# A hybrid retention and S5 step on one core: row order of the first loop, the norm's broadcast, and where the Toeplitz area is cleared

## The chip, the cores and the metric

The kernel runs on one core of one Trainium2 chip. The metric is the device time of one execution in microseconds (us), the median of several runs; the span is the time from the first to the last instruction in one profiled execution. Engines are called PE (matrix products), DVE (VectorE), ACT (ScalarE), POOL (GpSimd) and SP (SyncE, which only issues transfers here). Transfers are issued on the queues of SP, ACT and POOL.

## What is computed

One inference step of one layer, in float32, for a prompt of 1024 tokens and 8 single sample tokens, together 1032 token columns:

```python
h = rmsnorm(x, g_pre)                       # over d_model = 2048
q, k, v, za, ub, zb, ga, gb = split(h @ w_in)
ya, s_ret_new = retention(q, k, v, pos, s_ret)          # 8 heads of 128, chunks of 128
ya = (ya * silu(za)) @ w_pa
yb, s_re, s_im = s5(ub, ...)                # 64 groups of 16 channels, 64 complex states each
yb = (yb * silu(zb)) @ w_pb
out = (sigmoid(ga) * ya + sigmoid(gb) * yb) @ w_out
y = x + rmsnorm(out, g_post)
```

The outputs are y for both groups of tokens and the new states of the retention and of the S5 branch.

## The kernel before

All activations lie transposed: 128 channels on the partitions, tokens along the free axis. `xT` is x in 16 row tiles of 128 x 1032 (`KD` = 16). Each float32 operand is split into a high part, a rounded copy made by ACT, and a low part, the difference made by DVE; a product is the sum of three products of such parts (function `three`, lines 227 to 229, and line 952 in the main loop).

**First loop** (from line 382). It takes the row tiles k = 0 to 15. For each, SP loads the row (three buffers `xr`), ACT casts it times `g_pre` and DVE makes the low part; ACT squares the row (three buffers `sq`) and DVE adds the squares to `ssq`. PE at once multiplies the row with two column tiles of `w_in` (`M_UB`, `M_UB + 1`), three thirds of the tokens each. The 1/rms factor `rstd` isn't known yet, so these two results are kept unscaled and scaled later (`scale_ub`).

**The norm** (`first_rms`, `rms_bcast`). PE sums `ssq` over the partitions into a 128 x 9 tile, DVE adds epsilon, POOL takes the power -1/2, DVE multiplies an identity by the result (tile `st`, line 306), and PE multiplies a constant matrix with it, which broadcasts `rstd` to all partitions; DVE copies it out (line 317). Four 128-token chunks are done at a time, in three rounds.

**The forms** (`build_forms`). The main loop multiplies 2 x 2 blocks with seven products instead of eight, and needs seven combinations ("forms") of the scaled rows for each half of K: `u1`, `v1`, `v2` are pieces of the scaled rows, `t1` to `t4` are sums and differences of them, made in four `fo` buffers. They are stored to memory (`fm_d`) and read again later. For `kh` = 0 this works on rows 0 to 7 in four pairs (j, j + 4): POOL loads the rows again (buffers `fx`), DVE scales them (line 428) and makes the `t` forms, ACT issues the seven stores (line 438). For `kh` = 1 it does so with rows 8 to 15 in steps 1 to 3 of the main loop.

**Order of work.** `slot()` runs the next piece, up to a `yield`, of the first generator in the list `bg`; the projections call it at fixed places. While `linear` computes the third and fourth column tiles, there are four slots for each quarter of K: one behind each third of the tokens, and one behind the quarter. The high and low weights (`whi`, `wlo`) rotate through three pairs of tiles, `a`, `b` and `c`; the weights of the next quarter are asked for at the start of a quarter (`fetch_w`). The order on each engine is fixed before the run by a list scheduler that goes by priority (program order), readiness and a model of costs, so an instruction that depends on little can stand earlier in its engine's queue than in the program. `issue_after` keeps the pieces of a slot behind the last weight cast, weight difference or matmul of that engine. Each engine works through its queue in order.

**Main loop.** Steps of seven products of 24 matmuls each; `at(g, f)` runs f behind product g. `fetch(s + 1)` asks on SP's queue for the weights of the next step, in product 1 of a step; there are seven buffers `wr`.

**S5.** From step `B0 + 3` = 9 the S5 parameters are computed (`s5_params`), from step `B0 + 6` = 12 the 16 batches of four groups (`s5_all`, with `s5_mats`, `s5_phase`, `s5_toep` and others). A batch builds Toeplitz matrices by writing kernel rows into `t_d` in memory at staggered offsets and reading them back as 128 x 128 blocks; the part that stays zero, 112 columns of each row, must be cleared first. `s5_mats` does this for each batch: POOL clears a tile `zz` (line 621) and stores it, broadcast, to the batch's rows (line 622). All batches use the same place for `zz`. `s5_mats` also loads the batch's coefficients `bc` on POOL's queue (line 618), which DVE uses first in line 626. DVE in addition evacuates PE's accumulators, into `u2`, `u3` and others.

Of the kernel before, what the change touches and what calls it, by code (L numbers as in the profile page):

```python
# [79 lines left out]
def emit(ctx, tc, I, O):  # L80
# [27 lines left out]
    def st_tile():  # L108
        return stage_of["pool"].tile([128, stage_of["w"]], F32, name="st")
# [114 lines left out]
    def three(ps, w, i, x, t0, t1, first, last):  # L224
        wh, wl = w
        xh, xl = x
        T.matmul(ps, wh[:, i, :], xh[:, t0:t1], start=first, stop=False)  # L227
        T.matmul(ps, wh[:, i, :], xl[:, t0:t1], start=False, stop=False)  # L228
        anchor["p"] = T.matmul(ps, wl[:, i, :], xh[:, t0:t1], start=False, stop=last).ins  # L229
# [6 lines left out]
    def misc():  # L236
        return banks_of["pms"].tile([128, 512], F32, name="misc")
# [87 lines left out]
    def x_of(k):  # L325
        return xs[k][:, 0, :], xs[k][:, 1, :]
# [48 lines left out]
    ubw = ubstack.enter_context(tc.tile_pool(name="ubw", bufs=3))  # L375
    rm = ubstack.enter_context(tc.tile_pool(name="rm", bufs=1))
    ssq = rm.tile([128, TOK], F32, name="ssq")

    with tc.tile_pool(name="start", bufs=3) as sp:
        banks = [[mmbank() for _ in range(3)], [mmbank(), mmbank(), misc()]]  # L380
        w = None
        sqs = deque()
        for k in range(KD):
            xr = sp.tile([128, TOK], F32, name="xr")
            xh, xl = x_of(k)
            parts = THIRDS[0:3] if k == 0 else [(0, TOK)]
            for n, (a, b) in enumerate(parts):
                nc.sync.dma_start(xr[:, a:b], I["xT"][k, :, a:b])
                if k % 4 == 0 and n == 0:
                    w = [wquarter(w_in, M_UB, k // 4)]  # L390
                if k % 4 == 0 and n == len(parts) - 1:
                    w.append(wquarter(w_in, M_UB + 1, k // 4))
                A.activation(xh[:, a:b], xr[:, a:b], AF.Copy, scale=gpre[:, k:k + 1])
                V.scalar_tensor_tensor(xl[:, a:b], xr[:, a:b], gpre[:, k:k + 1], xh[:, a:b].bitcast(F32), ALU.mult, ALU.subtract)
            if k == 0:
                A.activation(ssq, xr, AF.Square)
            else:
                sqs.append(sp.tile([128, TOK], F32, name="sq", bufs=3))
                A.activation(sqs[-1], xr, AF.Square)
            for j in range(2):  # L400
                for t, (t0, t1) in enumerate(THIRDS[0:3]):
                    three(banks[j][t][:, 0:t1 - t0], w[j], k % 4, x_of(k), t0, t1, k == 0, k == KD - 1)
            if k > 1:
# [8 lines left out]
    def build_forms(kh, pool, fxs, fos, pre, after=()):  # L412
        raw = {}

        def load(j):
            for n in range(2):
                k = 8 * kh + j + 4 * n
                raw[k] = pool.tile([128, TOK], F32, name="fx", bufs=fxs)
                P.dma_start(raw[k], I["xT"][k])

        for j in range(pre):
            load(j)
        yield
        for j in range(4):
            t = {}
            for n, k in (("u", 8 * kh + j), ("v", 8 * kh + 4 + j)):
                r = raw.pop(k)
                V.scalar_tensor_tensor(r, r, gpre[:, k:k + 1], rstd, ALU.mult, ALU.mult)
                t[n + "1"], t[n + "2"] = r[:, 0:HT], r[:, HT:TOK]
            yield  # L430
            for n, a, b, op in (("t1", "u1", "u2", ALU.subtract), ("t3", "u2", "v2", ALU.subtract),
                                ("t2", "v2", "t1", ALU.add), ("t4", "v1", "t2", ALU.subtract)):
                t[n] = pool.tile([128, HT], F32, name="fo", bufs=fos)
                tt(t[n], t[a], t[b], op)
                if n == "t3":
                    yield
            for p, n in enumerate(FORMS):
                A.dma_start(fm_d[kh, p, j], t[n])
            yield
            if j and j + pre - 1 < 4:  # L440
                load(j + pre - 1)
            if j < len(after):
                after[j]()
            yield

    def first_rms():
        yield
        yield from rms_bcast(ssq, rstd, rm, 1)

    fb = ubstack.enter_context(tc.tile_pool(name="fb", bufs=1))  # L450
    forms_a = build_forms(0, fb, 6, 4, 3, (lambda: scale_ub(0), lambda: scale_ub(1)))
    next(forms_a)
    bg.append(first_rms())
    bg.append(forms_a)
    todo.extend((w_in, m, kq) for m in (M_UB + 2, M_UB + 3) for kq in range(4))
    todo.append((w_in, 16, 0))
    for j in (2, 3):
# [155 lines left out]
    def s5_mats(b):  # L613
        g0 = 4 * b
        pp = s5p
        d = s5d[b] = {}
        bc = W("bc", [128, 4, 64])
        P.dma_start(bc, I["bc"][:, g0:g0 + 4, :])
        rows = t_d.rearrange("(g r) x -> r g x", r=128)[:, g0:g0 + 4]
        zz = W("zz", [128, 112])  # L620
        P.memset(zz, 0.0)
        P.dma_start(rows[:, :, 0:112], zz.unsqueeze(1).broadcast_to([128, 4, 112]))
# [3 lines left out]
        V.tensor_scalar(b2, bs, sgn[:, 0:1], None, ALU.mult)  # L626
# [160 lines left out]
    def s5_all():  # L787
        yield from s5_mats(0)
        yield from s5_phase(0)
        for _ in range(3):  # L790
            yield
        s5_w1(0)
        yield
        for b in range(17):
            if b:
                s5_read(b - 1)
            if b < 16:
                s5_toep(b)
# [597 lines left out]
    for s in range(N2):  # L1396
        kh, p = steps[s]
        if s == 1:
            drain()
            gstack.close()  # L1400
            fstack, fb2 = popen("fb2", "left", 1)
            bg.append(build_forms(1, fb2, 4, 4, 2))
        if s == B0 - 2:
            drain()
            fstack.close()
# [518 lines left out]
```

## Time and profile before

| | |
|---|---|
| median of 3 runs | 2546.28 us (2543.64 to 2547.61) |
| profiled execution | 2549.9 us |
| its span | 2548.1 us, mean granted PE clock 0.995 |
| busy in the span | PE 2503.8, DVE 2010.5, ACT 996.7, POOL 781.2 us |
| moved by DMA | 530.77 MB, mean 208 GB/s |

Busy times are sums over the span; a wait is idle time of an engine together with what ended it, written "engine line <- releaser: us in total, times, longest us". In a timeline or chain the first two numbers are the start and the duration in us, counted from the span's start. Where a row ends in square brackets, they hold the idle time of the engine just before, and its releaser. In a row of windows, behind the stretch and its length, stand the busy times of PE, PE's weight loads, DVE, ACT and POOL with their counts of instructions, then PE's granted clock, the busy share of the 16 DMA engines, and GB/s. A row of DMA issues ends in the KB of one and the median us from issue to landing; a row of queues names packets, MB and the share of 16 engines' span.

### The profile page before, as it was taken

Reading aid. Unit: us, or ns where it says so; the run is one execution under the profiler, and the core shown is the slowest. Engines: PE = TensorE matmul, PEld = TensorE weight load, DVE = VectorE, ACT = ScalarE, POOL = GpSimd, SP = SyncE. Lnnn points to the kernel's source line nnn. Section 1 sums busy time; section 2 is a strip of 40 time slices with the busy share of each in tenths; the row PEclk is TensorE's granted clock in tenths of the full one; section 3 lists DMA queues with packets and bytes.
Section 4 is the critical chain, followed back from the end, with each engine's and each line's share of the span. In section 5 each row is a group of like instructions: output and inputs, shape, how many; then the busy total and the mean of one; then the engine's idle time right before and its main releaser. Section 6 shows DMA issues by size and latency. Waiting matters only on the chain.

```text
span 2548.1 us, 52901 instructions
## 1 busy us (share of the span) xinstructions
PE 2503.8 (98%) x20026; PEld 2456.2 (96%) x20026; DVE 2010.5 (79%) x4212; ACT 996.7 (39%) x1787; POOL 781.2 (31%) x1308
## 2 busy tenths in 40 slices
PE   9899998999999999999999999999999999999998
PEld 8899998999999999999999999999999999999976
DVE  7567777988988988767986676667897878989875
ACT  7042532333333333353334434444552432445532
POOL 0121334222222222223335434443332222433320
PEclk9999999999999999999999999999999999999999
DMA  7769676344444344688889988888888689857784
GB/s 242 245 212 308 190 176 172 126 136 131 127 136 128 118 139 125 200 221 213 213 217 265 236 227 228 206 234 226 279 285 289 216 238 318 291 191 174 210 300 142
DMA packets 238559, 530.77 MB, mean 208 GB/s; under 512 B 34928, under 2 KB 62016, under 8 KB 237536
## 3 DMA queue, kind: packets, MB, share of 16 engines
q0 software_dynamic: 106080, 310.20, 42.7%
q1 hardware_dynamic: 93280, 162.47, 20.2%
q10 hardware_dynamic: 38944, 54.71, 6.7%
q8 instruction: 158, 2.59, 0.4%
q14 instruction: 97, 0.79, 0.1%
HBM read 351.88 MB, written 175.37 MB: 207 GB/s over the span
## 4 chain that ended last, share of the span: by engine, by line
PE 81%; issue 6%; DMA 6%; DVE 4%; POOL 3%; ACT 0%; POOLq 0%; DVEq 0%; ACTq 0%; SPq 0%
PE acc L952 67%; PE acc L1822 3%; PE mm L229 1%; PE mm L227 1%; PE mm L228 1%; DMA t_d<-a 1%; DMA fm_d<-fo 1%; DVE a L85 1%; DMA a<-in_xT 1%; PE misc L782 1%; PE misc L781 1%; DVE u L85 1%; PE misc L1177 1%; PE misc L1187 1%; PE misc L1156 1%
## 5 line engine op out<-in xcount | busy, mean ns | idle before, releaser
L952 PE MATMUL acc<-a,whib 128*128 128x256 f32 (+1 forms) x3816 | 631.9, 285 | 15.3 <-DVE u L85 13.7
L952 PE MATMUL acc<-a,whic 128*128 128x256 f32 (+1 forms) x3808 | 629.1, 284 | 2.8 <-DVE u L85 2.2
L952 PE MATMUL acc<-a,whia 128*128 128x256 f32 (+1 forms) x3800 | 627.3, 284 | 0.5 <-ACT whia L933 0.5
L952 PEld LDWEIGHTS acc<-a,whib 128*128 128x128 f32 x3816 | 528.1, 189 | 18.2 <-DVE u L85 11.8
L952 PEld LDWEIGHTS acc<-a,whic 128*128 128x128 f32 x3808 | 525.2, 188 | 8.2 <-issue 2.8
L952 PEld LDWEIGHTS acc<-a,whia 128*128 128x128 f32 x3800 | 524.6, 188 | 2.2 <-issue 1.0
L952 PE MATMUL acc<-a,wlob 128*128 128x256 f32 (+1 forms) x1908 | 398.2, 283 | 0.4 <-DVE wlob L85 0.4
L952 PE MATMUL acc<-a,wloc 128*128 128x256 f32 (+1 forms) x1904 | 396.4, 283 | 0.4 <-DVE wloc L85 0.4
L952 PE MATMUL acc<-a,wloa 128*128 128x256 f32 (+1 forms) x1900 | 395.2, 283 | 0.0
L952 PEld LDWEIGHTS acc<-a,wlob 128*128 128x128 f32 x1908 | 299.4, 189 | 0.8 <-DVE wlob L85 0.6
L952 PEld LDWEIGHTS acc<-a,wloc 128*128 128x128 f32 x1904 | 297.7, 188 | 1.3 <-DVE wloc L85 1.2
L952 PEld LDWEIGHTS acc<-a,wloa 128*128 128x128 f32 x1900 | 297.3, 188 | 0.0
L933 ACT CAST whib<-wraw 128x512 fp32r<-128x512 f32 x146 | 90.7, 621 | 241.2 <-PE acc L952 190.0
L933 ACT CAST whic<-wraw 128x512 fp32r<-128x512 f32 x148 | 92.0, 621 | 236.2 <-PE acc L952 173.0
L933 ACT CAST whia<-wraw 128x512 fp32r<-128x512 f32 x146 | 90.8, 622 | 223.3 <-PE acc L952 164.9
L85 DVE TENSOR_TENSOR wraw<-wr 128x512 f32<-128x512 f32 x220 | 150.9, 686 | 2.6
L85 DVE TENSOR_TENSOR wloc<-wraw,whic 128x512 fp32r<-128x512 f32 x156 | 106.9, 685 | 51.6 <-ACT whic L933 39.8
L933 ACT CAST whib<-wr 128x512 fp32r<-128x512 f32 x111 | 68.9, 621 | 197.4 <-PE acc L952 152.6
L85 DVE TENSOR_TENSOR a<-stg,a 128x516 fp32r<-128x516 f32 (+1 forms) x224 | 135.9, 639 | 12.5 <-ACT a L274 8.3
L85 DVE TENSOR_TENSOR wloa<-wraw,whia 128x512 fp32r<-128x512 f32 x154 | 105.4, 685 | 46.7 <-ACT whia L933 31.7
L933 ACT CAST whia<-wr 128x512 fp32r<-128x512 f32 x110 | 68.3, 621 | 186.3 <-PE acc L952 158.0
L933 ACT CAST whic<-wr 128x512 fp32r<-128x512 f32 x109 | 67.7, 621 | 185.5 <-PE acc L952 165.7
(458 smaller groups left out, 4252.0 us busy)
## 6 DMA issues: line engine op xcount, KB each, us to landing
wr<-in_w_in SPq DMA_DIRECT2D x296, 256.0 KB
pt_d<-u POOLq DMA_DIRECT2D x74, 258.0 KB, 3.4
u<-pt_d POOLq DMA_DIRECT2D x74, 258.0 KB, 4.6
wr<-in_w_out SPq DMA_DIRECT2D x64, 256.0 KB
wr<-in_w_outB SPq DMA_DIRECT2D x64, 256.0 KB
stg<-fm_d POOLq DMA_DIRECT2D x60, 258.0 KB, 4.1
pt_d<-st POOLq DMA_DIRECT2D x37, 258.0 KB, 3.6
pt_d<-p POOLq DMA_DIRECT2D x37, 258.0 KB, 3.0
```

Of the source, the lines that this page charges most:

```text
L85: return (eng or V).tensor_tensor(out, a, b, op)
L227: T.matmul(ps, wh[:, i, :], xh[:, t0:t1], start=first, stop=False)
L228: T.matmul(ps, wh[:, i, :], xl[:, t0:t1], start=False, stop=False)
L229: anchor["p"] = T.matmul(ps, wl[:, i, :], xh[:, t0:t1], start=False, stop=last).ins
L781: T.matmul(o, Tm[:, g, :], U[:, g, 0:136], start=True, stop=False)
L782: T.matmul(o, W3[:, g, 1:9, :], X[:, g, 0:136], start=False, stop=True)
L933: anchor["a"] = A.copy(hi, f).ins
L952: anchor["p"] = T.matmul(o, a[:, i, :], x, start=first and i == 0 and a is wh and b is xh, stop=n in (2, 5, 6) and i == 3 and a is wl, ski ...
L1156: T.matmul(ps[:, c * 128:(c + 1) * 128], kt[:, 4 * i + c, :], vt[:, 4 * i + c, :], start=True, stop=True)
L1177: T.matmul(ps[:, c * 128:(c + 1) * 128], kT[:, cs], qT[:, cs], start=True, stop=True)
L1187: T.matmul(o, S[:, n], vt[:, n], start=True, stop=n == 0)
L1822: anchor["p"] = T.matmul(ps[c], a, b, start=k == 0 and a is xh and b is wh, stop=k == KD - 1 and a is xl).ins
```

## The change

- The first loop takes the rows in the order 8 to 15, 0, 3, 1, 2, 4, 5, 6, 7, in six buffers (pool `fxa`) instead of three. The last six rows, 1, 2, 4, 5, 6 and 7, stay there for `build_forms(0, ...)`; rows 0 and 3 are loaded again on POOL's queue when a pair is done. The pairs are taken in the order 1, 2, 0, 3. The squares have two buffers instead of three.
- `build_forms` stores `u1`, `v1`, `v2` one slot earlier than the `t` forms; for the first half these three go on POOL's queue, the others stay on ACT's.
- `first_rms` has its own code: the norm's sums in the first slot (before: the second), both diagonal tiles in the second, the two large broadcasts in the fourth and the small one in the fifth.
- The Toeplitz area is cleared once, by one tile `z0` and four stores on SP's queue, in products 1 to 4 of step `B0 + 3`; `s5_mats` clears nothing any more. The three empty slots in front of the first batch's `s5_w1` stand behind the first `bc` load instead.

```diff
+    fx = ubstack.enter_context(tc.tile_pool(name="fxa", bufs=6))
+    FX_ORDER = list(range(8, KD)) + [0, 3, 1, 2, 4, 5, 6, 7]
+    kept = {}
...
-        for k in range(KD):
-            xr = sp.tile([128, TOK], F32, name="xr")
+        for z, k in enumerate(FX_ORDER):
+            xr = kept[k] = fx.tile([128, TOK], F32, name="fx")
...
-                sqs.append(sp.tile([128, TOK], F32, name="sq", bufs=3))
+                sqs.append(sp.tile([128, TOK], F32, name="sq", bufs=2))
...
+                if n == "t3":
+                    for p, f in enumerate(FORMS):
+                        if f in ("u1", "v1", "v2"):
+                            eng.dma_start(fm_d[kh, p, j], t[f])
                     yield
             for p, n in enumerate(FORMS):
-                A.dma_start(fm_d[kh, p, j], t[n])
-            yield
-            if j and j + pre - 1 < 4:
-                load(j + pre - 1)
+                if n[0] == "t":
+                    A.dma_start(fm_d[kh, p, j], t[n])
+            yield
+            load(raw, z + 1)
...
+    def reload_a(raw, z):
+        if z in (1, 2):
+            k = 3 * (z - 1)
+            raw[k] = fx.tile([128, TOK], F32, name="fx")
+            P.dma_start(raw[k], I["xT"][k])
...
     def first_rms():
-        yield
-        yield from rms_bcast(ssq, rstd, rm, 1)
+        n_ch = [(c, min(c + 128, TOK)) for c in range(0, TOK, 128)]
+        r = TOK % 128
+        ps = misc()
+        for i, (a, b) in enumerate(n_ch):
+            T.matmul(ps[0:b - a, i:i + 1], ssq[:, a:b], onesk, start=True, stop=True)
...
+        P.tensor_tensor(rs, ms, hf, ALU.pow)
+        yield
+        dg = [st_tile()[:, 0:512] for _ in range(2)]
+        for i, d in enumerate(dg):
+            V.scalar_tensor_tensor(d.rearrange("p (j c) -> p j c", c=128), ident.unsqueeze(1).broadcast_to([128, 4, 128]), float(D),
+                                   rs[:, 4 * i:4 * i + 4].unsqueeze(2).broadcast_to([128, 4, 128]), ALU.mult, ALU.mult)
+        yield
+        yield
+        for i, d in enumerate(dg):
+            pb = misc()
+            T.matmul(pb, onesk.broadcast_to([128, 128]), d, start=True, stop=True)
+            V.tensor_copy(rstd[:, 512 * i:512 * i + 512], pb)
+        d = st_tile()[0:r, 0:r]
+        V.tensor_scalar(d, ident[0:r, 0:r], rs[0:r, 8:9], float(D), ALU.mult, ALU.mult)
+        yield
+        pb = misc()
+        T.matmul(pb[:, 0:r], onesk[0:r, :].broadcast_to([r, 128]), d, start=True, stop=True)
+        V.tensor_copy(rstd[:, SEQ:TOK], pb[:, 0:r])
+        yield
...
-    forms_a = build_forms(0, fb, 6, 4, 3, (lambda: scale_ub(0), lambda: scale_ub(1)))
-    next(forms_a)
     bg.append(first_rms())
-    bg.append(forms_a)
+    bg.append(build_forms(0, (1, 2, 0, 3), reload_a, fb, 4, P, (lambda: scale_ub(0), lambda: scale_ub(1))))
...
-        rows = t_d.rearrange("(g r) x -> r g x", r=128)[:, g0:g0 + 4]
-        zz = W("zz", [128, 112])
-        P.memset(zz, 0.0)
-        P.dma_start(rows[:, :, 0:112], zz.unsqueeze(1).broadcast_to([128, 4, 112]))
+        if b == 0:
+            for _ in range(3):
+                yield
...
         yield from s5_phase(0)
-        for _ in range(3):
-            yield
         s5_w1(0)
...
             bg.append(s5_params())
+            z0 = s5q.tile([128, 112], F32, name="z0")
+            P.memset(z0, 0.0)
+            for q in range(4):
+                at(7 * s + 1 + q, lambda q=q: nc.sync.dma_start(t_d.rearrange("(g r) x -> r g x", r=128)[:, 16 * q:16 * q + 16, 0:112],
+                                                               z0.unsqueeze(1).broadcast_to([128, 16, 112])))
```

More of the change, by code (lines that the diff above doesn't have):

```diff
@@ L382, in emit @@
         sqs = deque()
-        for k in range(KD):
-            xr = sp.tile([128, TOK], F32, name="xr")
+        for z, k in enumerate(FX_ORDER):
+            xr = kept[k] = fx.tile([128, TOK], F32, name="fx")
             xh, xl = x_of(k)
-            parts = THIRDS[0:3] if k == 0 else [(0, TOK)]
+            parts = THIRDS[0:3] if z == 0 else [(0, TOK)]
             for n, (a, b) in enumerate(parts):
                 nc.sync.dma_start(xr[:, a:b], I["xT"][k, :, a:b])
-                if k % 4 == 0 and n == 0:
+                if z % 4 == 0 and n == 0:
                     w = [wquarter(w_in, M_UB, k // 4)]
-                if k % 4 == 0 and n == len(parts) - 1:
+                if z % 4 == 0 and n == len(parts) - 1:
                     w.append(wquarter(w_in, M_UB + 1, k // 4))
@@ L394, in emit @@
                 V.scalar_tensor_tensor(xl[:, a:b], xr[:, a:b], gpre[:, k:k + 1], xh[:, a:b].bitcast(F32), ALU.mult, ALU.subtract)
-            if k == 0:
+            if z == 0:
                 A.activation(ssq, xr, AF.Square)
             else:
-                sqs.append(sp.tile([128, TOK], F32, name="sq", bufs=3))
+                sqs.append(sp.tile([128, TOK], F32, name="sq", bufs=2))
                 A.activation(sqs[-1], xr, AF.Square)
@@ L401, in emit @@
                 for t, (t0, t1) in enumerate(THIRDS[0:3]):
-                    three(banks[j][t][:, 0:t1 - t0], w[j], k % 4, x_of(k), t0, t1, k == 0, k == KD - 1)
-            if k > 1:
+                    three(banks[j][t][:, 0:t1 - t0], w[j], k % 4, x_of(k), t0, t1, z == 0, z == KD - 1)
+            if z > 1:
                 add(ssq, ssq, sqs.popleft())
@@ L410, in emit, with build_forms @@
     FORMS = ("u1", "t2", "v1", "t3", "t1", "t4", "v2")
[L412 to L422, printed above, removed]
+    def build_forms(kh, order, load, pool, fos, eng, after=()):
+        raw = dict(kept) if not kh else {}
+        load(raw, 0)
         yield
-        for j in range(4):
+        for z, j in enumerate(order):
             t = {}
@@ L442, in build_forms, with load_b @@
-            if j < len(after):
-                after[j]()
+            load(raw, z + 1)
+            if z < len(after):
+                after[z]()
             yield
-    def first_rms():
-        yield
-        yield from rms_bcast(ssq, rstd, rm, 1)
+    def reload_a(raw, z):
[3 more added lines that the diff above has]
+            P.dma_start(raw[k], I["xT"][k])
+    def load_b(raw, z):
+        for j in {0: (0, 1), 2: (2,), 3: (3,)}.get(z, ()):
+            for k in (8 + j, 12 + j):
+                raw[k] = fb2.tile([128, TOK], F32, name="fx", bufs=4)
+                P.dma_start(raw[k], I["xT"][k])
@@ new lines, in first_rms @@
+    def first_rms():
+        n_ch = [(c, min(c + 128, TOK)) for c in range(0, TOK, 128)]
[3 more added lines that the diff above has]
+            T.matmul(ps[0:b - a, i:i + 1], ssq[:, a:b], onesk, start=True, stop=True)
+        ms, rs, hf = (rm.tile([128, 9], F32, name=n) for n in ("ms", "rs", "hf"))
+        V.memset(ms, 1.0)
+        V.memset(hf, -0.5)
+        V.tensor_scalar(ms[:, 0:8], ps[:, 0:8], EPS, None, ALU.add)
+        V.tensor_scalar(ms[0:r, 8:9], ps[0:r, 8:9], EPS, None, ALU.add)
+        P.tensor_tensor(rs, ms, hf, ALU.pow)
+        yield
+        dg = [st_tile()[:, 0:512] for _ in range(2)]
[15 more added lines that the diff above has]
+        yield
@@ L1401, in emit @@
             fstack, fb2 = popen("fb2", "left", 1)
-            bg.append(build_forms(1, fb2, 4, 4, 2))
+            bg.append(build_forms(1, range(4), load_b, fb2, 4, A))
         if s == B0 - 2:
```

## The prediction

> **What bounds the kernel now.** I read the busy table first, then TensorE's (PE's) list of waits, then the chain of waits and the engine timelines around the two long ones.
>
> ```profile
> span 2548.1 us, 52901 instructions
> PE 2503.8 (98%) x20026; PEld 2456.2 (96%) x20026; DVE 2010.5 (79%) x4212; ACT 996.7 (39%) x1787; POOL 781.2 (31%) x1308
> PE acc L952 <- DVE u L85: 15.9, 8, 10.6
> PE mm L229 <- DVE wloa L85: 8.1, 1, 8.1
> PE mm L227 <- ACT whib L220: 4.9, 1, 4.9
> ```
>
> PE is busy for 98% of the span, and the diff changes no matmul of the projections, so only PE's waits can be won. They are two: one of 8.1 us and one of 10.6 us. The 4.9 us is the start, before the first weights are cast; the change leaves it.
>
> The first wait, by the chain of waits, VectorE's (DVE's) timeline and the 10 us windows:
>
> ```profile
> 87.71 12.69 DMA fm_d<-fo
> 75.36 2.49 DVE L428 SCALAR_TENSOR_TENSOR fx<-fx,g_pre,rstd 128x1032 f32<-128x1032 f32 x2
> 96.91 0.70 DVE L85 TENSOR_TENSOR fo<-fx 128x516 f32<-128x516 f32 x1 [4.00 <-DMA fm_d<-fo]
> 101.11 0.68 DVE L85 TENSOR_TENSOR wloa<-wraw,whia 128x512 fp32r<-128x512 f32 x1
> DVE fo L85 <- DMA fm_d<-fo: 7.7, 5, 4.0
> 70.00:80.00 10.00, 10.00 (x56) 8.74 (x55) 8.74 (x13) 0.62 (x1) 0.47 (x1) 1.00 0.28 101
> 80.00:90.00 10.00, 10.00 (x66) 10.00 (x65) 9.36 (x16) 0.62 (x1) 0.67 (x2) 1.00 1.02 309
> 90.00:100.00 10.00, 3.75 (x26) 3.43 (x24) 4.31 (x7) 0.62 (x1) 1.82 (x5) 0.95 1.04 312
> 102.54 0.32 PE mm L227
> 105.74 0.24 PE mm L227
> 106.50 0.18 PE mm L228
> ```
>
> DVE writes the forms into four `fo` buffers; each must be stored before it is reused. From 80 us on the transfers fill the 16 DMA engines (share 1.02 and 1.04, against 0.28 just before), so the stores land late, DVE stands 7.7 us in five waits, and the low half of the weights (`wloa`), queued behind, comes at 101.11. One store alone is 12.69 us of the chain. After the wait, matmuls run at 0.32 instead of 0.18 us, from the end of that subtraction, 101.8, until 105.74: 3.9 x (1 - 0.18/0.32) = 1.7 us. Cost of the first wait: 8.1 + 1.7 = 9.8 us.
>
> The second, by the timelines of POOL, DVE and PE and the list of waits around it:
>
> ```profile
> POOL a L621 <- DMA t_d<-a: 16.9, 10, 2.7
> L622 POOL DMA_DIRECT2D t_d<-a x16: 750/760/790, 356.2 to 426.4; - x16
> 408.26 0.92 POOL L618 DMA_DIRECT2D bc<-in_bc  x1
> 408.26 4.84 DMA bc<-in_bc
> 398.73 0.19 DVE L85 TENSOR_TENSOR phi<-phi,u 128x32 f32<-128x32 f32 x1
> 413.23 0.26 DVE L626 TENSOR_SCALAR a<-bc,sgn 128x64 f32<-128x64 f32 x1 [11.90 <-DMA bc<-in_bc]
> 418.88 1.23 PE L952 MATMUL acc<-a,whib 128*128 128x256 f32 x4 [10.62 <-DVE u L85]
> 423.76 0.64 PE L952 MATMUL acc<-a,whic 128*128 128x256 f32 x4
> 426.58 0.64 PE L952 MATMUL acc<-a,whia 128*128 128x256 f32 x4
> ```
>
> The zero stores of all 16 Toeplitz batches have drifted forward on POOL to 356 us. They share one zero tile, so each memset waits for the store before it (16.9 us in ten waits). The first `bc` load stands behind them, is issued at 408.26 and lands 4.84 us later. DVE, in order, waits 11.90 us for it, with the evacuation of PE's accumulator queued behind; PE stops for 10.62 us. The next product of 24 matmuls takes 418.88 to 423.76 = 4.88 us, the one after it 2.82: another 2.06. Cost: 12.7 us.
>
> **The Toeplitz area.** Sixteen memsets and sixteen POOL stores go; one memset and four stores on SyncE's (SP's) queue come, three steps earlier than the first batch. POOL is free, and `bc` can go out once DVE has finished the S5 parameters (398.92 by the row above, which ends their work), landing 4.84 us later, near 403.8. The moved pause puts three products (3 x 2.82 = 8.5 us) between the load's issue and DVE's first use, so DVE's evacuations pass ahead. Gain 12.7 us; a remainder would be at most the 4.84 us of that load, and I take none. What is late next: POOL's accumulating loads, whose waits were overlapped with PE all along.
>
> The four stores on SP's queue stand ahead of weight loads.
>
> ```profile
> t_d<-a POOLq DMA_DIRECT2D x16, 224.0 KB, 3.7
> DMA to landing us min/median/max: 2.5/3.7/6.0
> q1 hardware_dynamic: 93280, 162.47, 20.2%
> ```
>
> SP's queue (q1) moved 162.47 MB in 20.2% of 2548.1 us: 315 GB/s. The same 16 x 224 KB = 3.67 MB take 11.6 us there if alone; all 16 at the slowest landing would take 96. Weights are asked for four products (11.3 us) before use, and three of seven buffers are ahead of that. I take 0, the row of that queue being nearest; the ends are 0 and 96 - 11 = 85 us. Below nothing is excluded, as PE does not wait for these weights now. One memset by POOL ahead of them is 0.2 us.
>
> **The first loop.**
>
> ```profile
> 20.00:40.00 20.00, 20.00 (x129) 20.00 (x129) 18.76 (x19) 17.80 (x20) 0.00 (x0) 1.00 0.72 239
> 47.39 1.28 DVE L394 SCALAR_TENSOR_TENSOR a<-xr,g_pre,a 128x1032 fp32r<-128x1032 f32 x1
> 52.70 1.95 ACT L358 COPY ubp<-mm 128x384 f32<-128x384 f32 x3 [5.10 <-PE mm L229]
> 51.87 3.33 POOL L419 DMA_DIRECT2D fx<-in_xT  x6 [50.60 <-DVE ssq L85]
> 90.05 0.53 POOL L419 DMA_DIRECT2D fx<-in_xT  x1 [7.83 <-issue]
> ```
>
> The order of K changes nothing in the count: same loads, casts, squares, matmuls. Six row buffers instead of three let SP's loads run further ahead: nothing for PE, which is fully busy from 20 us. Two square buffers instead of three can stall ScalarE (ACT) and DVE: DVE has 20 - 18.76 = 1.24 us free in 20, so about 2.5 us over the loop is the bound; DVE's last split ends at 48.7 and the first evacuation waits for PE until 52.7, so that lag covers it. Without the cover it would cost those 2.5. I take 0, ends -1 and +1.
>
> Six loads of token rows on POOL go. They were issued at 51.87 and nobody waited; saved: nothing. The two that remain (rows 0 and 3) are as late as the two of before (the second at 90.05), and wait for a kept row to be stored.
>
> **The norm and the forms.**
>
> ```profile
> 61.29 1.83 POOL L295 TENSOR_TENSOR rs<-ms,hf 128x9 f32<-128x9 f32 x1 [6.08 <-DVE ms L294]
> 69.41 1.29 DVE L306 SCALAR_TENSOR_TENSOR st<-ident,rs 128x512 f32<-128x512 f32 x2
> 71.02 1.73 PE misc L314 x4
> 72.77 0.76 DVE rstd L317 x2
> 77.77 1.30 DVE L85 TENSOR_TENSOR fo<-fx 128x516 f32<-128x516 f32 x2
> ```
>
> The instructions are the same; their slots are fewer. Before, the broadcast finished in the ninth slot and the forms began in the tenth; now the fifth and the seventh. Four slots come in each quarter of a projection, 36 matmuls, and the row for 80 to 90 has 66 matmuls in 10 us: 5.5 us a quarter, 4.1 for three slots. The power ends at 61.29 + 1.83 = 63.1, and DVE takes up the diagonals 6.3 us later, at 69.41; if it goes at once, and the first slot's 1.4 us is won too, the forms begin 7.7 us sooner. I take 7: the diagonals now stand in the slot right behind the power. PE could wait for the diagonal tiles at the fourth slot: up to 1 us, taken 0.
>
> What that does to `wloa`: PE wants it at 101.8 - 8.1 = 93.7. Seven us earlier would bring 101.11 to 94.1, but the forms now stand three slots earlier in DVE's program, so a further row pair's scale and two differences (2.49 + 1.30 = 3.8) come ahead of it: 4.2 us late, before any change in the 7.7 us of store waits. Three of seven stores per pair leave ACT's queue for POOL's and are issued a slot sooner, and stores begin in the stretch where the DMA share is 0.28. If those waits go, PE's wait is 0; if they stay, 4.2, and if rows 0 and 3 come late too, the old 8.1. I take 2.4, between. Does such a wait cost clock? By the row of a short wait, yes:
>
> ```profile
> 2204.32 0.54 PE L952 MATMUL acc<-a,whib 128*128 128x324 f32 x2 [1.92 <-DVE u L85]
> 2206.00:2208.00 2.00, 2.00 (x9) 2.00 (x8) 2.00 (x5) 0.97 (x3) 0.55 (x1) 0.50 0.92 344
> ```
>
> After 1.92 us idle the granted clock was 0.50, so 1.7 is added again: 4.1 us left of 9.8, gain 5.7. The Trainium skill, page "TensorE: Matmul & The Clock Gate", Part 1, says that the clock falls after an idle window of about 3.4 us; by that a wait of 2.4 keeps full speed and the sum would be 1.7 us better, but this row, with 1.92 us, speaks against it.
>
> In the second half (steps 1 to 3) the raw stores go out one slot earlier on ACT, with the same number of instructions: 0.
>
> **Sum.** 12.7 + 5.7 = 18.4 us. The profiled execution's 2549.9 us stands 3.6 above the median of the runs, 2546.28; I take the gain off the median: 2527.9, say 2528.
>
> **Rivals.** (B) The forms' wait goes entirely: 12.7 + 9.8 = 22.5, 2523.8. For it: the idle DMA engines at 70 to 80; against: DVE has 9.36 us of work in 80 to 90. (C) It stays whole: the same bytes pass the same 16 engines, already full at 1.02, so moving three stores to another queue shortens no landing, and DVE waits for `fo` as before: 2533.6. The Trainium skill, "DMA: Bandwidth & Descriptors", section "Issuing engines are not separate DMA queues", states this rule: another issuer saves only issue time. The trace agrees as to the full share; that stores start earlier into idle engines speaks against it here. (D) The S5 change does not do what it says: DVE still meets the `bc` load and PE stops for its 4.84 us and 2.06 of slow clock, with half of the forms' gain: about 2546.3 - 5.8 - 2.8 = 2537.7. Against it: the pause of 8.5 us. (E) Slower: the zero stores hold SP's weights. It decides from 11.3 + 18.4 = 30 us of queue time on, 2.6 times the 11.6 worked out; at 60 us it is 2528 + 60 - 11 = 2577.
>
> **How the numbers follow.** Likeliest case 0.43, B 0.25, C 0.17, D 0.10, E 0.05. The range 2520 to 2538 takes in the first three and reaches to D; its lower end lies 3.8 us below B, for the lower end of the first loop and the spread of the runs (2543.64 to 2547.61). Outside are E and about half of D. About 0.2% (5.1 us) is what a measurement here can tell from no change. Faster: the first three, and most of D: 0.91; same 0.05; slower 0.04.
>
> **What would show it.** The wait on `bc` and PE's 10.6 us before line 952 gone, no zero stores on POOL after 350; `rstd` complete near 67 and the forms' first scaling near 68; PE's wait for a `wlo` tile under 5 us and DVE's waits on `fm_d` below 7.7; no PE wait on a weight cast in steps 9 to 12. Wrong would make it: `bc` still late because of what else POOL queues, DVE waiting for the reloaded rows 0 and 3, or weights late at step 10.

## The result and the profile after

| | before | after |
|---|---|---|
| median, measured together | 2544.96 us (2543.55 to 2547.61, 4 runs) | 2531.02 us (2529.45 to 2532.18, 4 runs) |
| profiled execution, its span | 2549.9, 2548.1 us | 2531.82, 2530.0 us |

The ratio is 0.9944, 95% interval 0.9926 to 0.9961: faster by 13.9 us between the medians, by 18.1 us between the two profiled executions. The forecast was 2528, 3.0 us lower, and the time lies in its range of 2520 to 2538.

The busy table and PE's list of waits, of the kernel after:

```profile
span 2530.0 us, 52856 instructions
PE 2499.5 (99%) x20026; PEld 2451.7 (97%) x20026; DVE 2010.4 (79%) x4212; ACT 998.1 (39%) x1787; POOL 770.0 (30%) x1283
PE mm L227 <- ACT whib L220: 5.0, 1, 5.0
PE acc L984 <- DVE u L85: 3.7, 5, 1.9
PE mm L229 <- DVE wloa L85: 3.0, 1, 3.0
PE mm L229 <- DVE wloc L85: 1.8, 1, 1.8
```

The wait of 10.6 us in S5 is gone; the sum of that kind of wait fell from 15.9 to 3.7 us. The forms' wait of 8.1 is not gone: it stands now in two pieces, 1.8 and 3.0. The matmul with the same number starts 12.66 us earlier after the S5 stretch than before it, relative to the kernel before, and only 1.7 us earlier after the stretch of the forms (56 to 112 us). The rest of the 18.1 us is 1.1 us before 56 us, 0.95 near 230, and shifts of about 1 us each way late in the span.

The S5 stretch of the kernel after, by POOL's and DVE's timelines and the windows:

```profile
395.55 0.57 POOL L653 DMA_DIRECT2D bc<-in_bc  x1 [0.72 <-DVE phi L85]
405.70 0.25 DVE L660 TENSOR_SCALAR a<-bc,sgn 128x64 f32<-128x64 f32 x1
395.00:405.00 10.00, 10.00 (x87) 10.00 (x87) 6.71 (x12) 2.92 (x6) 6.50 (x10) 1.00 0.95 193
405.00:415.00 10.00, 10.00 (x87) 10.00 (x87) 9.42 (x20) 2.42 (x5) 1.83 (x4) 1.00 0.61 193
```

`bc` is issued at 395.55, not 408.26, as soon as DVE has finished the parameters, and DVE comes to it 10 us later without a wait. PE is busy in every one of those 20 us at the full clock.

The forms of the kernel after, by DVE's timeline, DVE's waits from 62 to 115 us, PE's timeline, and windows of 2 us:

```profile
59.97 1.29 DVE L471 SCALAR_TENSOR_TENSOR st<-ident,rs 128x512 f32<-128x512 f32 x2 [1.94 <-POOL rs L467]
66.10 2.50 DVE L423 SCALAR_TENSOR_TENSOR fx<-fx,g_pre,rstd 128x1032 f32<-128x1032 f32 x2
87.75 0.68 DVE L85 TENSOR_TENSOR wloc<-wraw,whic 128x512 fp32r<-128x512 f32 x1
98.23 0.68 DVE L85 TENSOR_TENSOR wloa<-wraw,whia 128x512 fp32r<-128x512 f32 x1
DVE fo L85 <- DMA fm_d<-fo: 8.6, 6, 2.1
88.48 0.55 PE L229 MATMUL mm<-a,wloc 128*128 128x384 f32 x1 [1.82 <-DVE wloc L85]
98.96 0.69 PE L229 MATMUL mm<-a,wloa 128*128 128x384 f32 x1 [2.99 <-DVE wloa L85]
90.00:92.00 2.00, 2.00 (x7) 2.00 (x7) 1.58 (x2) 0.00 (x0) 0.12 (x1) 0.50 1.07 292
100.00:102.00 2.00, 2.00 (x7) 2.00 (x7) 1.11 (x2) 0.44 (x1) 0.00 (x0) 0.50 0.89 235
```

The forms begin at 66.10 instead of 75.36, 9.3 us sooner, yet the low weight `wloa` comes only 2.9 us sooner, at 98.23 instead of 101.11, and an earlier one, `wloc`, is late too. DVE's waits for the stores have not shrunk: 8.6 us in six, before 7.7 in five. Each of PE's two waits is followed by a stretch at a granted clock of 0.50.

### The profile page after: what moved, and what is told of

Read it like the earlier page. It is cut to its first block, busy times and chain, and to the rows that moved or that the text cites. A ratio compares the mean times of both kernels' runs of the same rounds, so it can differ in the third digit from the quotient of the medians.

```text
span 2530.0 us, 52856 instructions
## 1 busy us (share of the span) xinstructions
PE 2499.5 (99%) x20026; PEld 2451.7 (97%) x20026; DVE 2010.4 (79%) x4212; ACT 998.1 (39%) x1787; POOL 770.0 (30%) x1283
## 4 chain that ended last, share of the span: by engine, by line
PE 74%; issue 4%; DVE 3%; DMA 2%; POOL 2%; ACT 0%; ACTq 0%; POOLq 0%; DVEq 0%; SPq 0%
PE acc L984 66%; PE acc L1859 3%; DMA wr<-in_w_outB 1%; PE misc L816 1%; PE misc L815 1%; PE misc L1209 1%; PE misc L1219 1%; PE misc L1188 1%; DMA a<-in_xT 1%; PE misc L766 1%; POOL zr L1678 1%; DMA a<-mg_d 1%; PE misc L1221 0%; DVE a L85 0%; DVE u L85 0%
## 5 line engine op out<-in xcount | busy, mean ns | idle before, releaser
L85 DVE TENSOR_TENSOR a<-stg,a 128x516 fp32r<-128x516 f32 (+1 forms) x224 | 135.7, 637 | 10.6 <-ACT a L274 10.4
```

What stands on the lines that cost most here:

```text
L85: return (eng or V).tensor_tensor(out, a, b, op)
```

## The experiments

All times are medians. Each run is compared with runs of the kernel before on the same chip; where that differs from the table above, its median is given. The changed kernel was timed only beside the before of that table, its variants beside others, and the medians of the befores differ by up to 3.3 us; so smaller differences to the changed kernel are not shown by the medians alone.

### The Toeplitz part alone, in halves, and everything but it

Four kernels, against a before of 2547.57 us. `e1_toeplitz` is the kernel before with the whole Toeplitz part. `e2_pause` is the kernel before with the pause alone moved; the clearing stays on POOL for each batch. `e3_clear` is the kernel before with the clearing alone moved. `e4_rest` is the changed kernel with the Toeplitz part as it was.

```diff
# e1 = both hunks on the kernel before; e2 = the first; e3 = the second
+        if b == 0:                  # in s5_mats, behind the bc load
+            for _ in range(3):
+                yield
...
-        for _ in range(3):          # in s5_all, behind s5_phase(0)
-            yield
# second
-        zz = W("zz", [128, 112])
-        P.memset(zz, 0.0)
-        P.dma_start(rows[:, :, 0:112], zz.unsqueeze(1).broadcast_to([128, 4, 112]))
...
+            z0 = s5q.tile([128, 112], F32, name="z0")     # and its four stores on SP
```

> The kernel before with the Toeplitz part alone: one zero tile, four stores on SP's queue, no zero stores in the batches, and the pause of three slots moved behind the first bc load. Theory (the POOL queue of zero stores held the bc load, DVE and then PE): PE's wait of 10.6 us and its slow stretch of 2.1 us go, PE's wait of 8.1 us for wloa stays: 12.7 us faster than before, ratio 0.995. Rival (the first loop, the norm and the forms bring the most): under 5 us faster. Rival (zero stores on SP's queue delay weights): PE waits on weight casts in steps 9 to 12.

> The kernel before with only the pause of three slots moved behind the first bc load; the zero stores stay in the batches on POOL. Theory (POOL's queue is the cause): bc still lands near 413 us and DVE still stands in front of it; the pause lets about 8.5 us of DVE's other work pass ahead, so PE's wait shrinks from 10.6 to about 2 to 4 us: 6 to 8 us faster. Rival (the pause is what does it): PE's wait gone, 12.7 us faster, as with the clearing. Rival (the pause does nothing): 0.

> The kernel before with the clearing moved (one zero tile, four stores on SP's queue) and the pause left in its old place. Theory: bc is issued when DVE's parameter work ends, near 399 us, and lands by 404; DVE waits at most the 4.8 us of that load and PE, which has some slack, under 1 us: 12 us faster, within 1 us of the whole Toeplitz part. Rival (the pause is needed): PE waits 4 to 5 us and loses 2 us of clock: 6 us faster.

> The changed kernel without the Toeplitz part: new row order with kept rows, new norm broadcast, stores of u1, v1, v2 on POOL's queue, but zero stores and pause as before. Theory: PE's two waits of 1.8 and 3.0 us in the projections stay, the start and the forms give 2.8 us (difference of PE's progress between the two kernels by 160 us) and the second half of the forms 1 us; PE's wait of 10.6 us stays: 3 to 4 us faster. Rival (the parts need each other, so that their gains do not add): more than 8 us or none at all.

| | time | ratio (95%) | gain |
|---|---|---|---|
| e1, whole part | 2536.57 | 0.9957 (0.9942 to 0.9972) | 11.0 |
| e2, pause alone | 2539.67 | 0.9966 (0.9953 to 0.9978) | 7.9 |
| e3, clearing alone | 2537.98 | 0.9961 (0.9948 to 0.9974) | 9.6 |
| e4, all the rest | 2545.59 | 0.9990 (0.9981 to 0.9999) | 2.0 |

PE's waits, first of `e2`, then of `e3`, both from 395 to 440 us, then two rows of `e4` over its whole span:

```profile
PE acc L953 <- DVE u L85: 4.7, 1, 4.7
```

```profile
PE acc L948 <- DVE u L85: 0.8, 1, 0.8
```

```profile
PE acc L987 <- DVE u L85: 11.1, 6, 8.3
PE mm L229 <- DVE wloa L85: 4.3, 1, 4.3
```

The clearing on POOL was the cause: without it 0.8 us of the wait is left even with the pause in its old place. The pause alone hides part of the same wait and leaves 4.7. Together they leave none, and they overlap: 7.9 and 9.6 make 11.0. `e1` and `e4` add up to 13.0, near the 13.9 of the whole. So the Toeplitz part is the change's gain, and everything else brings about 2 us. Some expectations missed: `e1` was to gain 12.7 us, `e3` 12 and `e4` 3 to 4, and `e2`'s wait was to be 2 to 4 us. `e3` changes the place, the number and the queue of the zero stores together; which of the three is needed, no run separates.

### The norm alone, and everything but the norm

`e5_norm` is the kernel before with the new `first_rms` alone (before: 2546.03). `e11_oldnorm` is the changed kernel with the norm of before (before: 2548.22).

```diff
# e5, on the kernel before: the new first_rms.  e11, on the changed kernel: the old one
     def first_rms():
-        yield
-        yield from rms_bcast(ssq, rstd, rm, 1)
+        n_ch = [(c, min(c + 128, TOK)) for c in range(0, TOK, 128)]
...
```

> The kernel before with only the new norm broadcast (sums in the first slot, both diagonal tiles in the second, broadcasts in the fourth and fifth). Theory (the earlier norm is what the first half gains; the kept rows and POOL's stores bring nothing): rstd near 66 us instead of 73.5, forms end some 6 us sooner, PE's wait for a low weight shrinks from 6 to 8 us to about 5 in one or two pieces: 2 us faster, as much as all three edits of the first half together. Rival (the kept rows are needed for it, since the six loaded rows would still be on their way at 66 us): DVE waits for fx and nothing is gained: 0.

> The changed kernel with the norm's broadcast as it was before the change (three chained groups with a step of pause): kept rows, the new order of the first loop and the earlier stores stay. The new norm by itself made the kernel before 8.2 us slower, because the forms then came some steps earlier in VectorE's order and pushed the low weights behind three form rows. Theory (the gain before 110 us is one of the order of VectorE's work, and the parts belong together): without the new norm the forms start about 7 us later, near 73 to 75 us, the low weight is late again, and the time is 1 to 4 us above the changed kernel, 2532 to 2535 us. Rival (the norm part only moves the forms earlier, where they stand before the same stores): the same within 1 us, 2530 to 2532 us. Second rival (the norm part harms here too): faster than the changed kernel by 1 us or more, under 2530 us.

`e5` took 2554.27 us, ratio 1.0031 (1.0019 to 1.0043): 8.2 us slower, where neither side expected a loss. `e11` took 2532.18, ratio 0.9943 (0.9926 to 0.9959): 1.2 us above the changed kernel, within what these runs can tell, so its theory and its first rival stay undecided. POOL's and DVE's timelines of `e5` and PE's waits in it, then DVE's timeline of `e11`:

```profile
58.55 1.83 POOL L457 TENSOR_TENSOR rs<-ms,hf 128x9 f32<-128x9 f32 x1 [3.57 <-DVE ms L456]
68.16 0.69 DVE L85 TENSOR_TENSOR wlob<-wraw,whib 128x512 fp32r<-128x512 f32 x1 [4.89 <-ACT whib L220]
68.77 1.29 DVE L461 SCALAR_TENSOR_TENSOR st<-ident,rs 128x512 f32<-128x512 f32 x2
74.73 2.49 DVE L428 SCALAR_TENSOR_TENSOR fx<-fx,g_pre,rstd 128x1032 f32<-128x1032 f32 x2
95.86 0.68 DVE L85 TENSOR_TENSOR wloc<-wraw,whic 128x512 fp32r<-128x512 f32 x1
PE mm L229 <- DVE wloc L85: 7.5, 1, 7.5
PE mm L229 <- DVE wloa L85: 3.0, 1, 3.0
```

```profile
62.14 1.29 DVE L306 SCALAR_TENSOR_TENSOR st<-ident,rs 128x512 f32<-128x512 f32 x2 [1.94 <-POOL rs L295]
72.03 2.50 DVE L423 SCALAR_TENSOR_TENSOR fx<-fx,g_pre,rstd 128x1032 f32<-128x1032 f32 x2
```

In `e5` POOL's power is ready at 60.4 us, but the diagonals `st` stand behind two low weights in DVE's order, and the second waits 4.89 us for its cast; they start at 68.77, hardly sooner than before (69.41). So the forms begin 0.6 us sooner than before, while fewer slots have put three row pairs ahead of `wloc`, not two; it comes at 95.86 instead of 86.45. That is mostly the order of the work: from 74.73 to 95.86 DVE stands idle for only 2.75 us. In `e11`, with the old norm, the diagonals start at 62.14. So the kept rows and what comes with them (no reloads ahead of the norm, another order of the first loop, earlier stores) bring the diagonals ahead of the weights, not the new norm. That the six reloads, 3.33 us on POOL ahead of the power, set that place when the order was planned is my reading; no run separates them from the rest.

### What PE waits for at the forms

Three edits of the changed kernel, and two combinations. `e6_t3inplace` writes the form `t3` over `u2`, which nobody reads afterwards, so a pair needs three buffers, not four. `e7_act` issues the `u` and `v` stores of the first half on ACT's queue, not POOL's. `e8_ahead2` fetches the projections' weights two quarters ahead instead of one, so their casts and low parts stand earlier on ACT and DVE. `e9_both` is `e6` with `e8`, `e12_best` is `e7` with `e8`.

```diff
# e6
-                t[n] = pool.tile([128, HT], F32, name="fo", bufs=fos)
+                t[n] = t["u2"] if n == "t3" and not kh else pool.tile([128, HT], F32, name="fo", bufs=fos)
# e7
-    bg.append(build_forms(0, (1, 2, 0, 3), reload_a, fb, 4, P, ...))
+    bg.append(build_forms(0, (1, 2, 0, 3), reload_a, fb, 4, A, ...))
# e8, in wnext
-        if todo:
+        while todo and len(ahead) < 3:
             fetch_w()
```

> The changed kernel with t3 of the first half written over u2 instead of into an fo buffer, so that three forms of a pair share the four buffers. Theory (DVE stands before stores that still hold the four fo buffers, and the low weights stand behind it): DVE's 8.6 us of waits on fm_d fall below 3, PE's waits of 1.8 and 3.0 us and most of their 3.1 us of slow clock go: 5 to 8 us faster than the changed kernel. Rival (DVE's own work, not the buffers, is too much for the stretch): PE's waits move and shrink by less than a half: 0 to 3 us. Rival (rows 0 and 3 are reloaded later, since t3 holds its row longer): DVE waits for fx instead.

> The changed kernel with u1, v1, v2 of the first half stored on ACT's queue again. Theory (the 16 engines are full, so the queue does not matter): DVE's waits on fm_d stay between 7 and 10 us and the time within 1.5 us of the changed kernel. Rival (the prediction's reason: three of seven stores leave ACT's queue and the others land sooner): DVE's waits grow by 3 us or more, PE's waits with them: 3 to 5 us slower.

> The changed kernel with the weights of a projection asked for two quarters ahead instead of one, so that the low weights stand earlier in DVE's program. Theory (PE's wait is the place of the low weight in DVE's queue behind the forms): the low weights are made as soon as their pair is free, PE's waits of 1.8 and 3.0 us and the 3.1 us of slow clock go, while DVE's waits on fm_d stay near 8 us: 6 to 8 us faster than the changed kernel. Rival (DVE is too late for any order): the waits move to the evacuation of the accumulators: within 2 us.

> The changed kernel with both edits before together: the weights fetched two quarters ahead, and t3 written over u2 in the first half. Theory (what TensorE waits for at the low weights is their place in VectorE's order, behind forms that stand for the stores of earlier forms; each edit shortens one of the two): VectorE's wait for the stores stays at 1 to 2 us, its wait for the reloaded row at about 5 us, and TensorE waits under 1.5 us in all for low weights between 80 and 115 us; time 2524 to 2529 us. Rival (the reload that comes 5 us late now decides for the weights behind it, whatever their place): TensorE still waits 3 us or more for a low weight, 2530 to 2533 us. Second rival (the early start is given back by a later wait, as the look-ahead alone gave back 2 us by 156 us): no waits at 80 to 115 us, and still 2527 to 2530 us.

> The changed kernel with the weights fetched two quarters ahead, and the u and v forms of the first half stored on ScalarE's queue, not GpSimd's. Theory (the stores wait for the DMA engines, not for the queue, so the queue is worth 1 us at most; the look-ahead is worth 3 us): 2526 to 2529 us, TensorE's waits for low weights between 80 and 115 us under 2.5 us, and VectorE's wait for the stores 5 to 10 us. Rival (the two add up, since the stores on ScalarE's queue shortened VectorE's wait from 8.6 to 5.2 us): 2523 to 2526 us. Second rival (ScalarE's queue delays the casts that come earlier now): 2529 to 2533 us.

Store waits are DVE's on `fm_d` from 55 to 115 us, PE's waits those for weights from 60 to 115 us; the before of the first three is 2546.03 us, of the last two 2548.22.

| | time | ratio (95%) | DVE's store waits | PE's waits |
|---|---|---|---|---|
| after | 2531.02 | 0.9944 (0.9926 to 0.9961) | 8.6 | 1.8 + 3.0 |
| e6 | 2532.14 | 0.9945 (0.9930 to 0.9960) | 1.5 | 3.5 |
| e7 | 2530.43 | 0.9938 (0.9924 to 0.9953) | 5.2 | 3.4 |
| e8 | 2527.80 | 0.9925 (0.9909 to 0.9942) | 10.1 | 1.0 + 1.4 |
| e9 | 2526.19 | 0.9917 (0.9902 to 0.9932) | 4.4 and 1.1 before `wloc` | none |
| e12 | 2523.16 | 0.9905 (0.9890 to 0.9919) | 4.7 | none |

DVE's waits of `e6` from 55 to 115 us, then DVE's timeline and PE's windows of `e12`:

```profile
DVE fx L423 <- DMA fx<-in_xT: 5.3, 1, 5.3
DVE fo L85 <- DMA fm_d<-fo: 1.5, 2, 0.9
```

```profile
86.84 0.68 DVE L85 TENSOR_TENSOR wloa<-wraw,whia 128x512 fp32r<-128x512 f32 x1
94.55 0.70 DVE L85 TENSOR_TENSOR fo<-fx 128x516 f32<-128x516 f32 x1 [3.40 <-DMA fm_d<-fo]
96.12 0.69 DVE L85 TENSOR_TENSOR wlob<-wraw,whib 128x512 fp32r<-128x512 f32 x1
80.00:90.00 10.00, 10.00 (x65) 10.00 (x64) 10.00 (x17) 0.62 (x1) 1.27 (x4) 1.00 1.04 382
90.00:100.00 10.00, 10.00 (x66) 10.00 (x66) 4.44 (x6) 1.04 (x2) 0.00 (x0) 1.00 1.01 326
```

`e6` took away seven of the 8.6 us of store waits, and DVE waited 5.3 for a reloaded row instead, so a low weight still came late: with the buffers free, the transfer is the limit that ends last. `e8` left the store waits and moved the weights ahead of them in DVE's order; it gained 3.2 us by the medians, not the 6 to 8 expected. It kept two waits of PE, and the later one, 1.4 us, is for a cast on ACT, not for a low weight, and is followed by slow clock. In `e12` DVE still waits 4.7 us in full DMA engines (share 1.04 and 1.01), but `wloa` is made at 86.84, 11.4 us sooner than after, and PE does not stop. PE is 8.4 us ahead of the changed kernel at 112 us, and 8.5 at the end. So 8.4 us is what the change had left at the forms.

My expectation for `e12`, that the queue is worth 1 us at most, failed. With the weights ahead, moving the stores to ACT's queue was worth 4.6 us by the medians (the runs, 2526.19 to 2531.13 and 2521.72 to 2523.53, do not overlap), and it lowered the store waits both times: 8.6 to 5.2, 10.1 to 4.7. That is more than their spread: with the same code for the forms they are 8.7 in `e4` and 8.2 in `e10`. So `e7`'s first expectation, 7 to 10 us, failed too, though its time stayed within 1.5 us. Why one queue does better than two among full engines is open. `e9` also had more store waits than expected (4.4, not 1 to 2) and a shorter wait for the row (1.6, not 5), with the time in its range.

`e6` and `e7` show that a stretch can be won and the time not: by 112 us PE was 2.3 and 2.9 us ahead of the changed kernel's profile, and at the end 0.9 behind. `e7` lost 2.4 us near 1321 us, where it waited 2.03 us for an evacuated accumulator and then ran at a clock of 0.50 (the changed kernel: 1.20 us, full clock), and 0.6 or 0.7 us each near 230, 345 and 1927. `e6` lost 1.5 and 1.0 us near 1793 and 1926, about waits of 0.73 and 0.65 us, and 1.5 us near 2187, where a wait of 1.94 us was followed by slow clock; the changed kernel has the same wait of 1.94 us there and kept its clock. `e6` won back 1.1 us near 2445, in a wait that only the changed kernel has. On balance over the span `e9` gave back 2.4 us, 1.6 of it by slow clock at that place, and `e12` nothing. The last section shows what decides whether such a wait costs the clock; whether the edit or the execution makes the waits near 1793 and 1926, which the kernel before also has, is open.

`e12` beats both kernels: 2523.16 against 2531.02 and 2548.22 us.

### The zero stores on SP's queue, doubled

`e10_clear2` is the changed kernel with each zero store issued twice (before: 2548.22).

```diff
-            for q in range(4):
+            for q in (0, 0, 1, 1, 2, 2, 3, 3):
                 at(7 * s + 1 + q, ...)
```

> The changed kernel with each of the four zero stores on SyncE's queue issued twice, so that this queue carries 23.2 us more by the bytes (11.6 us of ring time once). Prediction (the queue has that much room in the step, so the clearing costs nothing there): same as the changed kernel within 1.5 us, 2529.5 to 2532.5 us, and no TensorE wait on a weight cast near 320 to 400 us. Rival E of the prediction (the stores hold up weights on that queue): TensorE waits of several us for a weight cast after the stores, 2534 us or more.

It took 2536.98 us, ratio 0.9960 (0.9946 to 0.9975): 6.0 us slower than the changed kernel. DVE's timeline and the windows of the changed kernel, then those of `e10`, with a row each of SP's, ACT's and PE's:

```profile
339.71 0.21 DVE L518 TENSOR_SCALAR e_t<-prm 128x96 f32<-128x96 f32 x1 [2.85 <-DMA prm<-in_prm]
326.00:336.00 10.00, 10.00 (x87) 10.00 (x87) 5.09 (x9) 3.63 (x6) 3.06 (x8) 1.00 0.90 240
336.00:346.00 10.00, 10.00 (x88) 10.00 (x87) 7.08 (x27) 5.85 (x8) 1.43 (x2) 1.00 0.53 100
```

```profile
331.30 4.28 SPq L1449 DMA_DIRECT2D t_d<-z  x2
337.45 1.24 ACTq L506 DMA_DIRECT2D prm<-in_prm  x1
346.29 0.21 DVE L518 TENSOR_SCALAR e_t<-prm 128x96 f32<-128x96 f32 x1 [7.70 <-DMA prm<-in_prm]
PE acc L984 <- DVE u L85: 4.3, 1, 4.3
326.00:336.00 10.00, 10.00 (x87) 10.00 (x86) 5.61 (x12) 4.83 (x7) 3.10 (x9) 1.00 1.10 327
336.00:346.00 10.00, 9.73 (x83) 9.53 (x81) 1.29 (x2) 4.05 (x6) 1.94 (x3) 1.00 1.06 254
```

The time is the rival's, its place is not: from 300 to 405 us PE waited for no weight. The doubled stores filled the DMA engines (1.10 and 1.06), so the S5 parameters `prm`, issued on ACT's queue, took 8.8 us to land, not 4.0; DVE stood 7.7 us for them, not 2.85, with PE's evacuation behind it, and PE stopped for 4.3. PE lost 5.8 us here by 380 us, 0.5 of which came back by 400; that is most of the 6.0. Issued once, the stores cost nothing that shows: from 300 to 405 us PE waits 0.3 us in the changed kernel, 0.5 before. The room for more is smaller than the 11.6 us of the bytes.

## Why the prediction was right or wrong

**The Toeplitz term** was 12.7 us and measured 12.66, through the steps that were given: POOL free, `bc` issued early, DVE's first use behind it. By medians, `e1` gave 11.0.

**The forms' term is the step that failed.** It put 4.1 us of 9.8 as left, from one wait of 2.4 us between 0 and 4.2, because the stores' waits "go" or "stay". (The 4.2 sets the start of `wloa`'s subtraction against the time at which PE wanted its end; with its 0.68 us it is 4.9.) They stayed, 8.6 us, and two weights were late instead of one, so the slow clock was paid twice. PE stood 1.82 + 2.99 us; then some ten matmuls took 0.32 us or more instead of 0.175, 1.6 us each time: 8.0 in all. `e12`, without these waits, won 8.4. The gain was 1.7 us between the profiles and 2.0 in `e4`, not 5.7. That a short wait costs the clock was read from one row; here it came true twice, but a wait of about this length could also have cost none, as the last section shows. Rival C's mechanism, bytes through full engines whatever the queue, was nearer for this term; its sum, 2533.6, is 2.6 us above the measured time, the forecast's 3.0 below. The rule of the Trainium skill that stood beside C ("DMA: Bandwidth & Descriptors", section "Issuing engines are not separate DMA queues"), that another issuer saves only issue time, agrees with the waits that stayed here, but not with `e7` and `e12`, where the issuer changed them by 3.4 and 5.4 us.

**The signs for the forms.** `rstd` was complete at 66.1 and the scaling began at 66.10 (forecast 67 and 68); PE's longest wait for a low weight was 3.0; the store waits did not fall. The start came out about right through wrong working. Seven us were credited to fewer slots, and removing the six loads was priced at "nothing, nobody waited". `e5` has the fewer slots with the loads and starts 0.6 us sooner, and `e11` has the old slots with the kept rows and starts 3.3 sooner; both together make 9.3.

**The sum and the median.** The profiles differ by 18.1 us, close to the 18.4 forecast, and that is luck: the 4.0 us missing at the forms are made up by the 1.1 us before 56 us, the 0.95 near 230 and the late shifts, which no term had. One of these, 1.3 us, is slow clock that the kernel before has behind its wait of 1.92 us at 2204 and the changed kernel, behind 1.94, has not. The whole gain of the profiled execution was taken off the median. But the forms' wait, unchanged in `e1`, `e2` and `e3`, was 6.5, 5.7 and 7.0 us in their profiles, 8.1 in the one that was read, which stood 3.6 us above the median. A part of the forecast gain was a long wait of that execution.

**First loop and zero stores** were put at 0. The 1.1 us before 56 us is less than `e10` lost there (1.4) with the same code. PE waited for no weight behind the zero stores, but they were weighed against SP's queue, and `e10` shows that the DMA engines, and through them a small load, are the nearer limit.

## What to carry to other kernels

When a low-priority chain and a critical cast share an in-order engine, ask first what stands ahead of the cast: moving the casts earlier halved PE's waits, and removed them together with either of the other edits, while a buffer saved or another queue alone only changed what was waited for. A part that starts sooner helps only if it does not also move ahead of something else; the norm alone cost 8.2 us. Price added transfers against every load that lands in the same stretch, whatever its queue, and take a gain off the median only as far as the wait is as long in other executions.

## What the hardware showed that was not expected

Whether the clock falls behind a wait of PE depends on where the wait lies, not on its length alone. After 1.54 us in `e4` it stayed at full speed, after 1.82 in the changed kernel it was 0.50. In `e8` it stayed full after 0.99 us and fell after 1.38, seven us later. The windows of `e4` behind its 1.54 us, then of `e8` behind each of its waits:

```profile
90.00:92.00 2.00, 2.00 (x13) 2.00 (x12) 1.28 (x2) 0.00 (x0) 0.42 (x1) 1.00 1.14 295
```

```profile
100.00:102.00 2.00, 2.00 (x13) 2.00 (x13) 0.69 (x1) 0.00 (x0) 0.00 (x0) 1.00 1.05 220
108.00:110.00 2.00, 2.00 (x8) 2.00 (x8) 2.00 (x6) 0.00 (x0) 0.00 (x0) 0.50 0.60 186
```

In each of the fourteen profiles all steps of the granted clock lie on one grid of 3.41 us, which begins at another place in each execution. Two windows of this grid in the changed kernel about its wait of 1.82 us, two about its wait of 1.94 at 2186 us, and two of `e9` about its wait of 1.96:

```profile
85.26:88.67 3.41, 1.59 (x12) 1.27 (x11) 1.30 (x2) 0.00 (x0) 0.79 (x2) 1.00 1.03 408
88.67:92.08 3.41, 3.41 (x12) 3.41 (x12) 1.90 (x2) 0.00 (x0) 0.20 (x1) 0.50 1.06 321
2181.04:2184.46 3.42, 2.96 (x21) 2.69 (x19) 1.40 (x4) 1.98 (x5) 2.57 (x5) 1.00 0.90 284
2184.46:2187.87 3.41, 1.93 (x13) 1.96 (x14) 3.41 (x8) 1.82 (x5) 0.62 (x2) 1.00 0.86 251
```

```profile
2177.23:2180.64 3.41, 1.45 (x11) 1.22 (x9) 2.17 (x5) 1.99 (x5) 1.60 (x3) 1.00 0.90 292
2180.64:2184.05 3.41, 3.41 (x15) 3.41 (x14) 3.41 (x8) 1.35 (x3) 0.54 (x1) 0.50 0.91 331
```

The 1.82 and the 1.96 us lie whole in one window, and the clock is 0.50 in the next; the 1.94 us is cut by the grid into 0.46 and 1.48, as `e4`'s 1.54 is into 0.93 and 0.61, and the clock stays. So it is in all fourteen profiles up to 30 us before PE's last matmul: the clock fell from full speed behind every window with 1.82 us or more of idle PE and behind none with 1.78 or less, but for one of 1.49 (in `e8`). `e12` even kept its clock through a wait of 2.12 us, of which 1.05 and 1.06 lay in two windows. Where the grid lies differs from execution to execution, so a wait of this length costs about 1.6 us more in one than in another; why the 1.49 was enough is open.

The Trainium skill ("TensorE: Matmul & The Clock Gate", Part 1) says that the clock falls after an idle window of about 3.4 us, that this window is free-running and does not start anew with a kernel, and that about 3.4 us of activity bring the clock back. The free-running window agrees with the grid, and the return agrees too: from 88.67 to 92.08 and from 98.91 to 102.32 us the clock was 0.50 in the changed kernel, 3.41 us each. That the whole window must be idle does not agree: 1.82 us of it were enough here.
